# Placing the operands of TensorE at multiples of 512 bytes in an encoder layer with a mixer and 16,384 experts

## The chip, the core and the metric

The kernel runs on one core of one Trainium2 chip. The metric is the device time of one execution in microseconds, from runs of the same program; the kernel before took 2557.3 us in the median of three runs (2555.47 to 2557.51). A profiled execution gives a trace with every instruction's start and duration.

## What is computed

One encoder layer on 256 tokens of width 2048, in float32. The reference, cut to its matrix products:

```python
mod = silu(c) @ w_ada + b_ada
sh1, sc1, g1, sh2, sc2, g2 = split(mod, 6)
h = x * (1 + sc1) + sh1
proj = h @ w_in
...
x = layer_norm(ALPHA * x + g1 * (concat([y_ssd, y_sc]) @ w_out))
h = x * (1 + sc2) + sh2
q = h @ w_query
...
u_sel = take(expert_u, idx); act = gelu(einsum('tkd,td->tk', u_sel, h))
v_sel = take(expert_v, idx); ffn = einsum('tk,tkd->td', act * gate, v_sel)
x = layer_norm(ALPHA * x + g2 * ffn)
```

The mixer between `w_in` and `w_out` is a bidirectional state-space scan in 32 heads beside a gated short convolution. The experts are 128 x 128 single neurons; each token takes 16 in each of 8 heads.

## The kernel before, in words

All large products are made to float32 accuracy from float32r parts. `wsplit` (L71 to L84) loads 512 KB of weights as `raw` (128 x 1024), ScalarE (ACT) rounds it into `hi` (L78), VectorE (DVE) takes the rest, `lo = raw - hi` (L81). The activations are split the same way. `mm3` (L89 to L93) multiplies three times: `hi` by the high part (L91), `hi` by the low part (L92), `lo` by the high part (L93). In `mm3` the weights are the stationary operand (128 columns of float32, 512 bytes in each partition) and 256 tokens are the moving operand (1024 bytes). The text calls these narrow matmuls.

The stages follow each other:

- 0 to 256 us: `mod` on VectorE from streamed `w_ada`, and the first columns of `w_in` (`ps`, `ps_b`, 1632 narrow matmuls).
- 256 to 658 us: the rest of `w_in` (`ps_in`, 2304 narrow), with the scan and the convolutions between. Every third chunk of `WHOLE` does its first half in plain float32 (`proj_whole`, L101); such a matmul is recorded as two instructions.
- 658 to 863 us: `w_out` (`ps_o`, 1536 narrow), whose moving operands are the mixer's 64 tiles `y`, then the first layer norm.
- 863 to 1071.5 us: `w_query` (`ps_q`, 1536 narrow) with the top-16 search on VectorE; most weights of this stage go through the pool `s3`.
- 1071.5 to 1816 us: all 128 groups of 128 experts are multiplied densely with `h` (`ps_u`, 6144 narrow matmuls). Up to about 1467 us the gates are spread over the experts beside this: one-hot tiles `eq`, scaled into `o2` on ScalarE, and two matmuls `ps_g` (L814) after each 24 narrow ones.
- 1816 us to the end: `expert_v` (`ps_v`, L878, L879, L881). Here the activations `ah`, `al` are stationary (512 bytes) and 512 columns of `hi` or `lo` are moving (2048 bytes): 3072 wide matmuls. Then the second layer norm.

Tiles come from pools. A pool opened on the left takes the next free bytes from the bottom of SBUF, one opened with `side="right"` from the top; each tile begins at a multiple of 32 bytes. `const` is opened first, `stream` (the buffers `raw`, `hi`, `lo` of most stages) next, so the sizes of the small tiles in `const` set where `stream` and all that lies above it begin. `h2p` (`h2h`, `h2l`, the split `h`) and `wk5` (`ah`, `al`) are at the top. A scheduler orders the instructions of each engine; SyncE (SP) issues all large DMAs in one queue.

Of the kernel before, what the change touches and what calls it, by code (L numbers as in the profile page):

```python
# [7 lines left out]
F32 = mybir.dt.float32  # L8
# [10 lines left out]
P = 128  # L19
S = 256  # L20
D = 2048
ND = D // P
# [18 lines left out]
def layer_kernel(ctx, tc, I, out, dbg=None):  # L41
    nc = tc.nc
    V, A, G, T = nc.vector, nc.scalar, nc.gpsimd, nc.tensor

    def dump(name, ap):
        if dbg and name in dbg:
            nc.sync.dma_start(dbg[name], ap)

    def pool(stack, name, bufs=1, **kw):
        return stack.enter_context(tc.tile_pool(name=name, bufs=bufs, reuse_waits="tile", **kw))  # L50

    const = pool(ctx, "const")
# [8 lines left out]

    iota = const.tile([P, NE], F32, name="iota")
    G.iota(iota, pattern=[[1, NE]], base=0, channel_multiplier=0, allow_small_or_imprecise_dtypes=True)
    eps_t = const.tile([P, 1], F32, name="eps_t")
    V.memset(eps_t, EPS)
    badaT = const.tile([P, 6, ND], F32, name="badaT")
    mod = const.tile([P, 6, ND], F32, name="mod")
# [62 lines left out]
    def log(dst, src):  # L130
        log_tables()
        with tc.issue_after(tables.ins):
            A.activation(dst, src, AF.Ln)
# [10 lines left out]
        return sq.ins, V.scalar_tensor_tensor(r, t, 1.5, r, op0=ALU.add, op1=ALU.mult).ins  # L144


    macc = const.tile([P, 2, 2, ND], F32, name="macc")

    def ada_half(scb, w, part, d, half):

        cs = slice(half * 1024, (half + 1) * 1024)
        V.scalar_tensor_tensor(w, w, 0.5, scb[:, cs], op0=ALU.mult, op1=ALU.mult,  # L152
                               accum_out=macc[:, half, part % 2, d:d + 1])
# [66 lines left out]
    prm = pool(st2, "prm")  # L220
# [5 lines left out]
        return ys[chunk]  # L226

    scb = prm.tile([P, D], F32, name="scb")
    par = prm.tile([P, 194], F32, name="par")
    at = 0  # L230

    def load(n, shape=None):
        nonlocal at
        t = par[:, at:at + n]
        at += n
        return t if shape is None else t.rearrange("p (a b) -> p a b", a=shape)

    dtb, alog = load(1)[:64], load(1)[:64]
    cw = load(72, 24)
    cb = load(24)  # L240
    scw = load(48, 16)
# [7 lines left out]

    H = 64  # L250
    acT = prm.tile([P, 2, H], F32, name="acT")
    lnT = prm.tile([P, 2, H], F32, name="lnT")
    nbT = prm.tile([P, 2, H], F32, name="nbT")
    offT = prm.tile([P, H], F32, name="offT")

# [31 lines left out]
        xt4.append(w0.tile([P, 4, S], F32, name="xt4", tag="xt4", bufs=2) if i < 2 else None)  # L287
    nc.sync.dma_start(xt4[0], I["xT"][:, 0:4])
    nc.sync.dma_start(par, I["par"])
    nc.sync.dma_start(lnp, I["lnp"])  # L290
    for half in range(2):
        cs = slice(half * 1024, (half + 1) * 1024)
# [49 lines left out]
    for d in range(ND):  # L342
# [6 lines left out]
        n = -(-len(units) // (4 - d % 4))  # L349
# [15 lines left out]
    wk = pool(st1, "wk", 2)  # L365

    def tmp(tag, shape=(P, S), bufs=2):
        return (wk if len(tag) > 2 else wkS).tile(list(shape), F32, name=tag, tag=tag, bufs=bufs)
# [76 lines left out]
    e1 = tmp("Emat", (P, 6, P))  # L445
# [3 lines left out]
    def dt_sums():  # L449
# [12 lines left out]
        V.scalar_tensor_tensor(dt, dt, 2.0, u, op0=ALU.mult, op1=ALU.mult)  # L462
        V.scalar_tensor_tensor(dt, xr, 0.0, dt, op0=ALU.max, op1=ALU.add)
        dump("dt", dt)
        aneg = prm.tile([H, 1], F32, name="aneg")
        A.activation(aneg, alog, AF.Exp)
        V.tensor_scalar(xr, dt, aneg, -1.0, op0=ALU.mult, op1=ALU.mult)

        V.tensor_scalar(u, dt, 1e-37, None, op0=ALU.max)
        log(u, u)  # L470
        adT = e1[:, 0:2, :H]
        yield
        yield
        for c in range(2):
# [27 lines left out]
        yield  # L502

    later.append(dt_sums())


# [129 lines left out]
    wk = pool(stK, "wk2", side="right")  # L636
# [34 lines left out]
    for d in range(ND):  # L671
        with tc.high_priority(offset=900):
            r = rT[:, d]
# [28 lines left out]
    gT = eTp.tile([P, 2, S], F32, name="gT")  # L702
    st3 = ExitStack()
    big = pool(st3, "big3")
    wk3 = pool(st3, "wk3", 2)
    s3 = pool(st3, "s3", 5)
    pq = pool(st3, "pq", 6, space=PSUM)
    psc = pool(st3, "psc", 2, space=PSUM)
    sk = big.tile([P, 8, 2, 2, NE], F32, name="sk")
# [16 lines left out]
    for h in range(8):  # L726
        qt = wk3.tile([P, 4, S], F32, name="qt", tag="qt")
        pss = [pq.tile([P, S], F32, name="ps_q", tag="pq") for _ in range(4)]
        for k in (range(0, 4, 4) if h == 0 else range(4)):
            n = 4 if h == 0 else 1  # L730
# [64 lines left out]
    with ExitStack() as p4:  # L795
# [32 lines left out]
        with ExitStack() as p4a:  # L828
            wk = pool(p4a, "wk4a", 2)
# [12 lines left out]
        wk = pool(p4, "wk4b")  # L842
# [13 lines left out]
    with ExitStack() as p5:  # L856
        wk = pool(p5, "wk5", side="right")
# [4 lines left out]
        nc.sync.dma_start(scb5, bass.AP(tensor=sc_d.tensor, offset=sc_d.offset, ap=[[0, P], [1, D]]))  # L862
        banks = [[pv.tile([P, 512], F32, name="ps_v", tag="pm") for _ in range(4)] for _ in range(2)]
        g2b = wk.tile([P, D], F32, name="g2b")
        st = wk.tile([P, 2, 16], F32, name="st")

        def a_pair(e2):
            ah = wk.tile([P, 2, S], F32R, name="ah", tag="ah", bufs=3)
# [107 lines left out]
def _layout(inp):  # L976
    import numpy as np

    n = {k: np.asarray(v) for k, v in inp.items()}
    r = {}  # L980
# [4 lines left out]
    r["w_ada"] = n["w_ada"][0].reshape(D, 6, ND, P).transpose(1, 2, 3, 0)  # L985
    r["c"] = n["c"]
    pad = lambda f, b: np.concatenate([f[0], b[0], np.zeros(64, f.dtype)])[:, None]
    r["par"] = np.concatenate([
        pad(n["dt_bias_f"], n["dt_bias_b"]), pad(n["a_log_f"], n["a_log_b"]),
        n["conv_ssd_w"][0].reshape(3, 24, P).transpose(2, 1, 0).reshape(P, 72), cols(n["conv_ssd_b"][0]),  # L990
        n["short_conv_w"][0].reshape(3, 16, P).transpose(2, 1, 0).reshape(P, 48),
        cols(np.repeat(n["d_skip"][0], 64)), cols(n["ssd_norm_g"][0]), cols(n["sc_norm_g"][0])], axis=1)
# [42 lines left out]
```

## Time and profile before

| | us |
|---|---|
| median of 3 runs | 2557.3 |
| lowest and highest run | 2555.47, 2557.51 |
| profiled execution | 2552.61 |
| its span, first to last instruction | 2550.7 |
| TensorE busy (95% of the span) | 2424.6 |
| VectorE busy (73%) | 1862.2 |
| ScalarE busy (54%) | 1381.3 |

The mean granted TensorE clock of the profiled execution is 0.984 of full speed. Busy times of engines overlap. Records of consecutive matmuls overlap as well: one takes 0.28 us from start to end while the next starts after 0.11 us, so the pace of TensorE is read from starts, first and last of a stretch with their count, and not from durations.

### The profile page before, as it was taken

The numbers are of one execution on the slowest core, as the hardware profiler recorded it, in microseconds if no ns is written. First come the engines' busy times: TensorE is split into PE (matmuls) and PEld (weight loads), VectorE is DVE, ScalarE is ACT, GpSimd is POOL, SyncE is SP. The second block draws the span as 40 slices with busy tenths as digits, with TensorE's granted clock in tenths as the row PEclk, the third lists the DMA queues.
The fourth block names the chain that finished last, engine by engine and source line by source line (L and its number), as shares of the span: only waits on it lengthen the run. The fifth ranks groups of instructions, "written<-read, shape, count | busy, mean of one in ns | idle before, by whom it ended". The sixth has DMA issues, their size and how long they took to land.

```text
span 2550.7 us, 44290 instructions
## 1 busy us (share of the span) xinstructions
PE 2424.6 (95%) x17122; PEld 2248.3 (88%) x17122; DVE 1862.2 (73%) x3255; ACT 1381.3 (54%) x2506; POOL 0.9 (0%) x7
## 2 busy tenths in 40 slices
PE   5889999999999899999999999999998999999997
PEld 5889888888899799999999999999886888888886
DVE  8788888989887799898888855555675555645545
ACT  3435476656444554499999944444443444544442
POOL 0000000000000000000000000000000000000000
PEclk9999999999999899999999999999999999999999
DMA  9886766778887565355666666666788655655554
GB/s 356 313 297 236 260 217 224 235 260 280 267 291 259 196 206 181 116 181 193 199 195 200 198 218 219 218 217 219 257 307 274 217 194 190 223 192 193 193 190 149
DMA packets 183252, 575.67 MB, mean 226 GB/s; under 512 B 22209, under 2 KB 44929, under 8 KB 182657
## 3 DMA queue, kind: packets, MB, share of 16 engines
q1 hardware_dynamic: 183042, 572.85, 67.3%
q8 instruction: 134, 2.20, 0.3%
q14 instruction: 76, 0.62, 0.1%
HBM read 560.10 MB, written 12.66 MB: 225 GB/s over the span
## 4 chain that ended last, share of the span: by engine, by line
PE 67%; DMA 15%; DVE 12%; ACT 3%; issue 2%; SPq 1%; DVEq 0%; ACTq 0%
PE ps_u L91 9%; PE ps_u L92 9%; PE ps_u L93 9%; PE ps_v L879 8%; PE ps_v L881 8%; PE ps_v L878 8%; DVE lo L81 5%; DMA adaw<-in_w_ada_dram 4%; DMA raw<-in_w_in_dram 3%; DMA big<-in_w_ada_dram 2%; ACT hi L78 2%; DVE adaw L152 2%; DMA raw<-in_w_inA_dram 2%; PE ps_q L93 2%; PE ps_q L92 2%
## 5 line engine op out<-in xcount | busy, mean ns | idle before, releaser
L81 DVE TENSOR_TENSOR lo<-raw,hi 128x1024 fp32r<-128x1024 f32 (+1 forms) x804 | 972.1, 1212 | 506.8 <-ACT hi L78 504.7
L78 ACT ACTIVATE hi<-raw 128x1024 fp32r<-128x1024 f32 (+1 forms) x804 | 843.6, 1051 | 884.6 <-PE ps_v L879 302.1
L91 PE MATMUL ps_u<-h2h,hi 128*128 128x256 f32 x2048 | 568.7, 278 | 0.0
L92 PE MATMUL ps_u<-h2l,hi 128*128 128x256 f32 x2048 | 568.1, 277 | 0.0
L93 PE MATMUL ps_u<-h2h,lo 128*128 128x256 f32 x2048 | 568.1, 277 | 0.0
L878 PE MATMUL ps_v<-hi,ah 128*128 128x512 f32 x992 | 390.1, 393 | 9.9 <-ACT hi L78 8.1
L879 PE MATMUL ps_v<-hi,al 128*128 128x512 f32 x992 | 390.7, 394 | 1.2 <-DVE al L120 1.2
L91 PEld LDWEIGHTS ps_u<-h2h,hi 128*128 128x128 f32 x2048 | 386.2, 189 | 0.0
L92 PEld LDWEIGHTS ps_u<-h2l,hi 128*128 128x128 f32 x2048 | 384.6, 188 | 0.0
L93 PEld LDWEIGHTS ps_u<-h2h,lo 128*128 128x128 f32 x2048 | 384.5, 188 | 0.0
L881 PE MATMUL ps_v<-lo,ah 128*128 128x512 f32 x992 | 268.9, 393 | 0.8 <-DVE lo L81 0.8
L878 PEld LDWEIGHTS ps_v<-hi,ah 128*128 128x128 f32 x992 | 187.5, 189 | 52.3 <-ACT hi L78 8.9
L879 PEld LDWEIGHTS ps_v<-hi,al 128*128 128x128 f32 x992 | 187.7, 189 | 43.0 <-DVE al L120 1.6
L91 PE MATMUL ps_in<-h2h,hi 128*128 128x256 f32 x768 | 222.3, 289 | 3.0 <-DVE mod L159 2.2
L881 PEld LDWEIGHTS ps_v<-lo,ah 128*128 128x128 f32 x992 | 186.8, 189 | 42.0 <-DVE lo L81 2.0
L93 PE MATMUL ps_in<-h2h,lo 128*128 128x256 f32 x768 | 217.6, 283 | 2.3 <-DVE lo L81 2.3
L152 DVE SCALAR_TENSOR_TENSOR adaw<-adaw,scb 128x1024 f32<-128x1024 f32 x160 | 193.1, 1219 | 35.3 <-DMA adaw<-in_w_ada_dram 35.0
L92 PE MATMUL ps_in<-h2l,hi 128*128 128x256 f32 x768 | 217.6, 283 | 0.0
L809 ACT ACTIVATE o<-eq,gT 128x128 fp32r<-128x128 f32 x512 | 161.4, 388 | 0.0
L91 PEld LDWEIGHTS ps_in<-h2h,hi 128*128 128x128 f32 x768 | 146.6, 191 | 9.0 <-issue 4.2
L93 PEld LDWEIGHTS ps_in<-h2h,lo 128*128 128x128 f32 x768 | 147.1, 191 | 4.6 <-DVE lo L81 2.9
L93 PE MATMUL ps_o<-y,lo 128*128 128x256 f32 x512 | 145.6, 284 | 5.0 <-DVE lo L81 4.9
(285 smaller groups left out, 3975.0 us busy)
## 6 DMA issues: line engine op xcount, KB each, us to landing
raw<-in_expert_u_dram SPq DMA_DIRECT2D x256, 512.0 KB, 4.5
raw<-in_expert_v_dram SPq DMA_DIRECT2D x248, 512.0 KB, 3.9
adaw<-in_w_ada_dram SPq DMA_DIRECT2D x160, 512.0 KB, 6.0
raw<-in_w_in_dram SPq DMA_DIRECT2D x110, 512.0 KB, 5.0
raw<-in_w_out_dram SPq DMA_DIRECT2D x64, 512.0 KB, 4.3
raw<-in_w_query_dram SPq DMA_DIRECT2D x64, 512.0 KB, 3.9
raw<-in_w_inB_dram SPq DMA_DIRECT2D x44, 512.0 KB, 4.4
big<-in_w_ada_dram SPq DMA_DIRECT2D x32, 512.0 KB, 5.6
```

The costliest lines, as they stand in the source:

```text
L78: A.activation(hi, raw, AF.Copy)
L81: V.tensor_tensor(lo, raw, hi.bitcast(F32), op=ALU.subtract)
L91: T.matmul(ps, wh, mh, start=start, stop=False)
L92: T.matmul(ps, wh, ml, start=False, stop=False)
L93: T.matmul(ps, wl, mh, start=False, stop=stop)
L152: V.scalar_tensor_tensor(w, w, 0.5, scb[:, cs], op0=ALU.mult, op1=ALU.mult, accum_out=macc[:, half, part % 2, d:d + 1])
L809: A.activation(o2[:, k], eq[:, i, 1].bitcast(F32), AF.Copy, scale=gT[:, k, t0 + i:t0 + i + 1])
L878: T.matmul(banks[tb][c], ah[:, ts], vh, start=start, stop=False)
L879: T.matmul(banks[tb][c], al[:, ts], vh, start=False, stop=False)
L881: T.matmul(banks[tb][c], ah[:, ts], vl, start=False, stop=stop)
```

## The change

The small tiles `macc`, `eps_t`, the two vectors of the step size (`dtb`, `alog`) and `aneg` become parts of one tile `top` of 120 floats, in a pool of its own at the upper end of SBUF. The two vectors leave the input `par` and arrive by a DMA of their own, `dtp`. `lnT` moves into the unused half of `e1`, `st` grows from 16 to 64 columns, and pool `s3` is opened ahead of `wk3`. No arithmetic changes.

```diff
--- before.py
+++ after.py
@@ -61,7 +61,9 @@
 
     iota = const.tile([P, NE], F32, name="iota")
     G.iota(iota, pattern=[[1, NE]], base=0, channel_multiplier=0, allow_small_or_imprecise_dtypes=True)
-    eps_t = const.tile([P, 1], F32, name="eps_t")
+
+    top = pool(ctx, "top", side="right").tile([P, 120], F32, name="top")
+    macc, eps_t, dtp = top[:, :64].rearrange("p (h a d) -> p h a d", h=2, a=2), top[:, 64:65], top[:, 72:74]
     V.memset(eps_t, EPS)
     badaT = const.tile([P, 6, ND], F32, name="badaT")
     mod = const.tile([P, 6, ND], F32, name="mod")
@@ -144,8 +146,6 @@
         return sq.ins, V.scalar_tensor_tensor(r, t, 1.5, r, op0=ALU.add, op1=ALU.mult).ins
 
 
-    macc = const.tile([P, 2, 2, ND], F32, name="macc")
-
     def ada_half(scb, w, part, d, half):
 
         cs = slice(half * 1024, (half + 1) * 1024)
@@ -226,7 +226,7 @@
         return ys[chunk]
 
     scb = prm.tile([P, D], F32, name="scb")
-    par = prm.tile([P, 194], F32, name="par")
+    par = prm.tile([P, 192], F32, name="par")
     at = 0
 
     def load(n, shape=None):
@@ -235,7 +235,7 @@
         at += n
         return t if shape is None else t.rearrange("p (a b) -> p a b", a=shape)
 
-    dtb, alog = load(1)[:64], load(1)[:64]
+    dtb, alog = dtp[:64, 0:1], dtp[:64, 1:2]
     cw = load(72, 24)
     cb = load(24)
     scw = load(48, 16)
@@ -249,7 +249,6 @@
 
     H = 64
     acT = prm.tile([P, 2, H], F32, name="acT")
-    lnT = prm.tile([P, 2, H], F32, name="lnT")
     nbT = prm.tile([P, 2, H], F32, name="nbT")
     offT = prm.tile([P, H], F32, name="offT")
 
@@ -287,6 +286,7 @@
         xt4.append(w0.tile([P, 4, S], F32, name="xt4", tag="xt4", bufs=2) if i < 2 else None)
     nc.sync.dma_start(xt4[0], I["xT"][:, 0:4])
     nc.sync.dma_start(par, I["par"])
+    nc.sync.dma_start(dtp, I["dtp"])
     nc.sync.dma_start(lnp, I["lnp"])
     for half in range(2):
         cs = slice(half * 1024, (half + 1) * 1024)
@@ -462,13 +462,13 @@
         V.scalar_tensor_tensor(dt, dt, 2.0, u, op0=ALU.mult, op1=ALU.mult)
         V.scalar_tensor_tensor(dt, xr, 0.0, dt, op0=ALU.max, op1=ALU.add)
         dump("dt", dt)
-        aneg = prm.tile([H, 1], F32, name="aneg")
+        aneg = top[:H, 80:81]
         A.activation(aneg, alog, AF.Exp)
         V.tensor_scalar(xr, dt, aneg, -1.0, op0=ALU.mult, op1=ALU.mult)
 
         V.tensor_scalar(u, dt, 1e-37, None, op0=ALU.max)
         log(u, u)
-        adT = e1[:, 0:2, :H]
+        adT, lnT = e1[:, 0:2, :H], e1[:, 0:2, H:]
         yield
         yield
         for c in range(2):
@@ -702,8 +702,8 @@
     gT = eTp.tile([P, 2, S], F32, name="gT")
     st3 = ExitStack()
     big = pool(st3, "big3")
+    s3 = pool(st3, "s3", 5)
     wk3 = pool(st3, "wk3", 2)
-    s3 = pool(st3, "s3", 5)
     pq = pool(st3, "pq", 6, space=PSUM)
     psc = pool(st3, "psc", 2, space=PSUM)
     sk = big.tile([P, 8, 2, 2, NE], F32, name="sk")
@@ -862,7 +862,7 @@
         nc.sync.dma_start(scb5, bass.AP(tensor=sc_d.tensor, offset=sc_d.offset, ap=[[0, P], [1, D]]))
         banks = [[pv.tile([P, 512], F32, name="ps_v", tag="pm") for _ in range(4)] for _ in range(2)]
         g2b = wk.tile([P, D], F32, name="g2b")
-        st = wk.tile([P, 2, 16], F32, name="st")
+        st = wk.tile([P, 2, 64], F32, name="st")
 
         def a_pair(e2):
             ah = wk.tile([P, 2, S], F32R, name="ah", tag="ah", bufs=3)
@@ -985,8 +985,8 @@
     r["w_ada"] = n["w_ada"][0].reshape(D, 6, ND, P).transpose(1, 2, 3, 0)
     r["c"] = n["c"]
     pad = lambda f, b: np.concatenate([f[0], b[0], np.zeros(64, f.dtype)])[:, None]
+    r["dtp"] = np.concatenate([pad(n["dt_bias_f"], n["dt_bias_b"]), pad(n["a_log_f"], n["a_log_b"])], axis=1)
     r["par"] = np.concatenate([
-        pad(n["dt_bias_f"], n["dt_bias_b"]), pad(n["a_log_f"], n["a_log_b"]),
         n["conv_ssd_w"][0].reshape(3, 24, P).transpose(2, 1, 0).reshape(P, 72), cols(n["conv_ssd_b"][0]),
         n["short_conv_w"][0].reshape(3, 16, P).transpose(2, 1, 0).reshape(P, 48),
         cols(np.repeat(n["d_skip"][0], 64)), cols(n["ssd_norm_g"][0]), cols(n["sc_norm_g"][0])], axis=1)
```

Where the two built programs place the tiles, as the start in a partition modulo 512 bytes:

| tile | before | changed |
|---|---|---|
| `raw`, `hi`, `lo` of pool `stream` (moving in `ps_v`, else stationary) | 288 | 0 |
| `raw`, `hi`, `lo` of pool `s3` (most of `ps_q`) | 32 | 0 |
| `h2h`, `h2l` (moving in `ps`, `ps_b`, `ps_in`, `ps_q`, `ps_u`) | 480 | 0 |
| `y` (moving in `ps_o`), `h2w` (moving in L101) | 352 | 0 |
| `ah`, `al` (stationary in `ps_v`) | 480 | 0 |
| `eq` (stationary) and `o2` (moving) in `ps_g` | 288 | 0 |
| `rT` | 224 | 256 |

TensorE's instructions stand in the same order in both programs; so do, names apart, those of VectorE and of POOL. Two places differ. On the DMA queue of SP, at the start of the program (`adaw` are the first tiles of `w_ada`, `xt` the first tile of `x`), before:

```order
L281 DMA adaw_145<-in_w_ada_dram 128x1024 x2
L284 DMA badaT<-in_b_adaT_dram 128x96
L288 DMA xt_149<-in_xT_dram 128x1024
L289 DMA par<-in_par_dram 128x194
L290 DMA lnp<-in_lnp_dram 128x32
L296 DMA sc_d<-scb 1x2048
```

And with the change:

```order
L280 DMA adaw_146<-in_w_ada_dram 128x1024 x2
L283 DMA badaT<-in_b_adaT_dram 128x96
L287 DMA xt_150<-in_xT_dram 128x1024
L288 DMA par<-in_par_dram 128x192
L289 DMA top<-in_dtp_dram 128x2
L290 DMA lnp<-in_lnp_dram 128x32
L296 DMA sc_d<-scb 1x2048
```

One DMA is added ahead of `lnp`; `par` is two floats shorter in each partition. On ScalarE, just after the first tile of `h` (`h2w` is `h` in float32, `top` at L466 is `aneg`), before:

```order
L294 ACTIVATE lo<-scb 128x1024 x2
L314 ACTIVATE h2w_129<-xt_149,mod 128x256
L466 ACTIVATE aneg<-par 64x1
L119 ACTIVATE h2h<-h2w_129 128x256
L128 ACT_TABLE_LOAD
```

And with the change:

```order
L294 ACTIVATE lo<-scb 128x1024 x2
L314 ACTIVATE h2w_130<-xt_150,mod 128x256
L121 ACTIVATE h2h<-h2w_130 128x256
L466 ACTIVATE top<-top 64x1
L130 ACT_TABLE_LOAD
```

The exponential of 64 numbers stands one place later, behind the first rounding.

## Rows read from the trace of the kernel before

**Rows 1.** The page: span, busy time by engine, the chain that ended last by engine.
```profile
span 2550.7 us, 44290 instructions
...
PE 2424.6 (95%) x17122; PEld 2248.3 (88%) x17122; DVE 1862.2 (73%) x3255; ACT 1381.3 (54%) x2506; POOL 0.9 (0%) x7
...
PE 67%; DMA 15%; DVE 12%; ACT 3%; issue 2%; SPq 1%; DVEq 0%; ACTq 0%
```

**Rows 2.** Windows by stage: length, then busy us (xinstructions), granted clock, DMA share.
```profile
core 0: us, PE busy (x) PEld busy (x) DVE busy (x) ACT busy (x) POOL busy (x), PEclk, DMA share, GB/s
0.00:256.00 256.00, 210.01 (x1640) 201.00 (x1641) 208.85 (x369) 109.23 (x163) 0.63 (x6) 0.97 0.83 300
256.00:658.00 402.00, 375.52 (x2767) 346.57 (x2766) 353.60 (x685) 254.93 (x541) 0.00 (x0) 0.97 0.73 246
658.00:863.00 205.00, 189.48 (x1548) 186.14 (x1546) 153.46 (x258) 88.28 (x118) 0.24 (x1) 0.97 0.80 266
863.00:1071.50 208.50, 198.51 (x1679) 196.44 (x1680) 197.23 (x653) 101.75 (x181) 0.00 (x0) 0.98 0.52 173
1071.50:1467.00 395.50, 393.05 (x3351) 389.92 (x3350) 339.51 (x588) 363.04 (x972) 0.00 (x0) 1.00 0.59 190
1467.00:1816.00 349.00, 348.64 (x3076) 348.44 (x3075) 200.26 (x257) 154.25 (x196) 0.00 (x0) 1.00 0.68 218
1816.00:2550.70 734.70, 709.39 (x3072) 579.79 (x3072) 409.29 (x448) 309.78 (x340) 0.00 (x0) 0.98 0.65 215
```

**Rows 3.** Instructions on tile ps_u, 1470 to 1810 us; third column first and last start.
```profile
L93 PE MATMUL ps_u<-h2h,lo x1001: 276/276/276, 1469.9 to 1809.9; 128*128 128x256 f32 x167
```

**Rows 4.** Instructions on tile ps_o, 802 to 855 us.
```profile
L93 PE MATMUL ps_o<-y,lo x150: 279/279/279, 801.8 to 854.4; 128*128 128x256 f32 x150
```

**Rows 5.** Instructions on tile ps_q, 978 to 996 us and 1004 to 1021 us.
```profile
L93 PE MATMUL ps_q<-h2h,lo x54: 276/276/276, 977.8 to 995.8; 128*128 128x256 f32 x54
...
L93 PE MATMUL ps_q<-h2h,lo x48: 281/281/281, 1004.0 to 1020.7; 128*128 128x256 f32 x48
```

**Rows 6.** Instructions on tile ps_v, 2100 to 2500 us.
```profile
L878 PE MATMUL ps_v<-hi,ah x584: 388/390/394, 2100.1 to 2499.7; 128*128 128x512 f32 x195
L879 PE MATMUL ps_v<-hi,al x584: 388/392/394, 2100.3 to 2499.9; 128*128 128x512 f32 x195
L881 PE MATMUL ps_v<-lo,ah x581: 388/394/394, 2099.8 to 2498.1; 128*128 128x512 f32 x194
```

**Rows 7.** Two windows at the lower clock, and timeline rows (start us, us) in each.
```profile
865.20:866.50 1.30, 1.30 (x8) 1.30 (x8) 1.30 (x4) 0.70 (x2) 0.00 (x0) 0.50 1.04 425
1823.60:1824.90 1.30, 1.30 (x4) 1.00 (x3) 0.54 (x1) 0.05 (x1) 0.00 (x0) 0.50 0.88 246
...
865.18 0.41 PE L93 MATMUL ps_q<-h2h,lo 128*128 128x256 f32 x1
...
866.46 0.41 PE L93 MATMUL ps_q<-h2h,lo 128*128 128x256 f32 x1
...
1824.06 0.63 PE L878 MATMUL ps_v<-hi,ah 128*128 128x512 f32 x1
1824.49 0.63 PE L879 MATMUL ps_v<-hi,al 128*128 128x512 f32 x1
```

**Rows 8.** The chain in order of time, 500 to 512 us: start, length, what.
```profile
506.89 3.45 PE ps_in L101 x16
```

**Rows 9.** Timeline of TensorE around a pair of gate matmuls, from 1301.18 us.
```profile
1301.18 0.28 PE L93 MATMUL ps_u<-h2h,lo 128*128 128x256 f32 x1
1301.29 0.39 PE L814 MATMUL ps_g<-o,eq 128*128 128x256 f32 x2
1301.53 0.28 PE L91 MATMUL ps_u<-h2h,hi 128*128 128x256 f32 x1
```

**Rows 10.** Groups by line on ACT, 900 to 1060 us, then 1500 to 1800 us.
```profile
L78 ACT ACTIVATE hi<-raw 128x1024 fp32r<-128x1024 f32 x52 | 55.0, 1059 | 45.5 <-PE ps_q L92 36.0 <-DMA raw<-in_w_query_dram 5.2 <-ACT qt L734 2.3
...
L78 ACT ACTIVATE hi<-raw 128x1024 fp32r<-128x1024 f32 x111 | 118.0, 1063 | 169.2 <-PE ps_u L92 167.6 <-DMA raw<-in_expert_u_dram 1.6
```

**Rows 11.** Timeline of the DMA queue, 6 to 9 us, and of ACT, 14 to 15 us.
```profile
6.40 0.33 SPq L290 DMA_DIRECT2D lnp<-in_lnp_dram  x1
8.75 0.30 SPq L296 DMA_DIRECT2D sc_d<-scb  x1
...
14.35 0.19 ACT L466 ACTIVATE aneg<-par 64x1 f32<-64x1 f32 x1
```

## Prediction, made before the changed kernel ran

> **What bounds the kernel now.** The page first: TensorE is busy for 95% of the span, and the chain that ended last is TensorE for 67%, DMA for 15% and VectorE for 12% [rows 1]. The windows by stage say where this average comes from [rows 2]. From 1467 us to the end TensorE is the bound alone: 348.6 of 349.0 us in the second part of the first expert product, then 709.4 of 734.7 us. From 1071.5 to 1467 us it has a companion, since ScalarE is busy for 363.0 of 395.5 us; in the query stage VectorE is busy for 197.2 of 208.5 us. In the three stages before, TensorE is idle for 46.0, 26.5 and 15.5 us, and DMA shares of 0.73 to 0.83 tell what it waits for. Gains in TensorE's pace come out whole only in the last two windows.
>
> Then the pace itself, read from first and last start with the count. Narrow matmuls (256 columns) follow each other on `ps_u` at 340.0 us / 1000 / 3 = 113.3 ns [rows 3], on `ps_o` at 52.6 / 149 / 3 = 117.7 ns [rows 4], and on `ps_q` at 113.2 ns in one stretch and 118.4 in another [rows 5]. Wide ones (512 columns, 1749 starts in 400.1 us) come every 228.9 ns [rows 6]. The columns alone would take 106.7 and 213.3 ns at 2.4 GHz. What is the rest? At the lower granted clock, 0.50 or 1.2 GHz, there is none: six narrow gaps take 1.28 us, 213.3 ns each, and a wide one takes 0.43 us, which is 512 columns and nothing else [rows 7]. At full clock the plain float32 matmuls of L101, which take 512 column times for 256 columns, come every 3.45 us / 16 = 215.6 ns [rows 8], only 2.3 ns over. So only streams that take a new float32 column in every cycle at 2.4 GHz pay more. With 2.3 ns as the unavoidable part, the floors are 109.0 ns narrow and 215.6 wide. Over them lie 4.3, 8.7 and 13.3 ns: one, two and three steps of some 4.4 ns.
>
> The reader should note two things. The moving tiles of `ps_o` start 352 bytes past a multiple of 512 and always pay two steps; `h2h` starts at 480 and pays one or two. That speaks for the address. But `ps_q` shows both paces with the same addresses, so the phase of loads against matmuls has a say too.
>
> **The change, part by part.** My reading: an operand that starts off a multiple of 512 touches one more 512-byte block than it needs, the moving and the stationary operand each, and each extra block can cost one step. A narrow matmul has two extra blocks and pays one or two steps; a wide one has two as well and pays three. With all starts at 0 the narrow ones come to 109.0 ns, the wide ones lose two of three steps and come to 220.0. No start at 0 is in this trace, so this is bounded only by the rows: at best the floor for both, and on the other side no gain or a loss (rivals).
>
> The sum, stage by stage, with the counts and busy times of [rows 2]:
>
> 1. 1467 to 1816 us: 3076 instructions x 4.3 ns = 13.2 us, whole.
> 2. 1816 us to the end: 3072 x 8.9 = 27.3 us, whole; 40.9 at the floor of 215.6.
> 3. 1071.5 to 1467 us: 395.5 us / 3351 = 118.0 ns for an instruction, waits and both paces together. At 109.0 it would be 365 us, 30 less, but ScalarE alone needs 363.0. It would have no slack for its gate work, so I take 20, which leaves it 97% busy.
> 4. 658 to 863 us: 1548 x 8.7 = 13.5 us. Up to about 800 us `w_ada` tiles compete for the DMA queue; I take two thirds, 9.
> 5. 256 to 658 us: 2304 narrow ones at 4.3 to 8.7 ns, on average 6.5, give 15 us; with VectorE at 88% and DMA at 0.73, half: 7.5. Behind a faster TensorE the raw weights are late next.
> 6. 863 to 1071.5 us: 1536 at 4.3 to 8.7 give 6.6 to 13.4 us, but VectorE (95% busy) is late next. I take 3.
> 7. Up to 256 us: 1632 x 6.5 = 10.6 us of TensorE time in a stage that waits for VectorE and DMA. I take 2.
>
> Together 82.0 us. Taking every stage at its upper end gives 13.2 + 40.9 + 30 + 13.5 + 15 + 13.4 + 10.6 = 137.
>
> The rest is near nothing. The added DMA `dtp` costs an issue of about 0.33 us like `lnp`'s; the queue is idle from 6.73 to 8.75 us behind `lnp` [rows 11], which hides it. Were that cover gone, 0.33 us would fall on the next loads of `w_ada`. `aneg`, 0.19 us [rows 11], runs after the first rounding instead of before it, which lets TensorE's first operand be ready no later. `lnT` in `e1`, the wider `st` and `s3` ahead of `wk3` add no instruction. That ScalarE and VectorE, or DMA, gain from rounder addresses too, I put at 0: the same ScalarE rounding takes 1059 ns on tiles at 32 (pool `s3`) and 1063 at 288 [rows 10], no sign of an effect.
>
> Against its own time the profiled execution would go from 2552.6 to 2470.6 us. The median of the runs, 2557.3, is 4.7 above that execution; on this scale the forecast is **2475 us**.
>
> **The rivals.** *Only one operand counts (faster, about 2509).* The weights may be fetched early enough that their extra block is free, or the other way round. Then a wide matmul loses one step, to 224.5 (3072 x 4.4 = 13.5 us), `ps_o` goes to 113.3 (4.5 after waits), the steady `ps_u` still reaches 109.0 if its one step is the one that goes (13.2), the mixed stretch gives 12, the other three 1.5, 3 and 1: 48.7 us in all. For it: `h2h` often pays one step with both its operands off. Against: three steps on wide matmuls are not explained by one operand. [...]
>
> *The start does not matter (no change, 2557).* The steps may be the price of feeding a column in every cycle, whatever its address; the absence at half the rate [rows 7, 8] fits that as well, and [rows 5] shows a pace changing with no address changed. Against it: `ps_o` keeps two steps through all its 150 groups of three [rows 4]. [...] That the change does not do what it says can be left out: the built program has all these tiles at 0.
>
> *Equal starts collide (slower, about 2622).* With the change moving and stationary operands start at the same place in their blocks. Ordered by the distance between the two starts before, the paces are: 448 (`ps_q`) and 192 (`ps_u`) one or two steps, 64 (`ps_o`) always two, and 0, which only the gate matmuls have (both at 288), two starts in 0.24 us, 120 ns each [rows 9]. If nearness is what costs, all narrow ones go to 120 and wide ones pay a fourth step: 3076 x 6.7 = 20.6 us, 3351 x 4.5 (from a mean of 115.5 between the two paces) = 15.1, 3072 x 4.4 = 13.5, 1548 x 2.3 = 3.6, then 7 in the query stage and 5 in `ps_in` after what VectorE and DMA hide: 65 us. It decides as soon as steady `ps_u` runs above 113.3. Against it: a pair of gate matmuls is also a change of operands and of accumulator, which could cost those nanoseconds by itself.
>
> **How the numbers follow.** 0.2%, 5 us, is what a measurement of this kernel can tell from no change. I give the forecast 0.40, one operand 0.26, no effect 0.18, collision 0.16; so faster 0.66, same 0.18, slower 0.16. The forecast's own range is 2440 to 2500: the low end adds to the 82 us the wide floor (13.6) and some 21 of the 41 us held back in the other stages. To hold 8 in 10 the range must reach over the second and third case and ends at 2562, the highest run plus the 5 us; the collision is left out.
>
> **What would show it right or wrong.** In the changed trace: starts on `ps_u` from the middle of its stage at 109 ns instead of 113.3 and no stretch at 117.7; `ps_o` at 109; wide matmuls near 220 (215.6 would be the best end, 224.5 the rival's, 233 the collision's); the last two windows shorter by 13 and 27 us, the mixed one by 20 with ScalarE then the busiest; the query stage nearly as long as before. The forecast is wrong if `ps_u` keeps 113.3 and 117.7, if the wide pace stays at 228.9, or if the gain appears in the first 256 us, where only DMA or VectorE could have made it.

## The result and the profile after

The change made the kernel slower: 2580.28 us in the median of four runs (2575.91 to 2583.03), against 2556.39 for four runs of the kernel before (2549.79 to 2557.51); the ratio is 1.0097, with a 95% interval of 1.0073 to 1.0121. The forecast of 2475 us had the wrong sign, and its range ended at 2562. The profiled execution took 2583.03 us, 30.4 more than that of before.

In the changed kernel the lines of `wsplit` and `mm3` stand two further down: `hi` is rounded in L80, `lo` taken in L83, the triple is L93, L94, L95, and `proj_whole` is L103. The page first: span, busy time by engine, the chain by engine.

```profile
span 2581.2 us, 44290 instructions
...
PE 2469.0 (96%) x17122; PEld 2298.3 (89%) x17122; DVE 1871.0 (72%) x3255; ACT 1393.9 (54%) x2506; POOL 0.9 (0%) x7
...
PE 69%; DMA 14%; DVE 11%; ACT 3%; issue 2%; SPq 1%; DVEq 0%; ACTq 0%
```

Beside [rows 1], TensorE took 44.4 us more for the same 17122 instructions. Where? These are the windows of the changed kernel, cut where the same work begins and ends as in [rows 2] (columns as there).

```profile
0.00:253.60 253.60, 212.09 (x1637) 203.64 (x1638) 210.35 (x370) 109.21 (x162) 0.63 (x6) 0.95 0.85 304
253.60:653.00 399.40, 382.58 (x2769) 354.46 (x2768) 354.32 (x685) 255.15 (x542) 0.00 (x0) 0.98 0.74 248
653.00:857.50 204.50, 190.06 (x1547) 186.53 (x1545) 152.18 (x256) 88.30 (x118) 0.24 (x1) 0.99 0.80 265
857.50:1073.00 215.50, 207.74 (x1679) 205.63 (x1680) 198.03 (x654) 102.85 (x182) 0.00 (x0) 0.97 0.52 168
1073.00:1480.00 407.00, 405.54 (x3354) 403.01 (x3353) 346.54 (x589) 374.66 (x973) 0.00 (x0) 1.00 0.57 185
1480.00:1849.50 369.50, 368.86 (x3074) 368.66 (x3073) 200.29 (x257) 154.14 (x195) 0.00 (x0) 1.00 0.64 206
1849.50:2581.20 731.70, 702.11 (x3072) 576.38 (x3072) 409.25 (x448) 309.59 (x340) 0.00 (x0) 0.99 0.66 216
```

Stage by stage the change is -2.4, -2.6, -0.5, +7.0, +11.5, +20.5 and -3.0 us, together the 30.5 by which the span grew. The loss lies in the three windows of `ps_q` and `ps_u`; `w_in` and `w_out` did not grow, and the wide matmuls at the end gained a little.

The pace explains it. Instructions on tile `ps_u` in the part without gates, and TensorE's timeline around a pair of gate matmuls:

```profile
L95 PE MATMUL ps_u<-h2h,lo x973: 283/283/283, 1490.0 to 1839.9; 128*128 128x256 f32 x195
```
```profile
1308.11 0.28 PE L95 MATMUL ps_u<-h2h,lo 128*128 128x256 f32 x1
1308.23 0.40 PE L814 MATMUL ps_g<-o,eq 128*128 128x256 f32 x2
1308.47 0.28 PE L93 MATMUL ps_u<-h2h,hi 128*128 128x256 f32 x1
...
1311.35 0.40 PE L814 MATMUL ps_g<-o,eq 128*128 128x256 f32 x2
```

The first row gives 349.9 / 972 / 3 = 120.0 ns where [rows 3] gave 113.3. In the second view 24 narrow matmuls take 1311.35 - 1308.47 = 2.88 us, 120.0 each, and the gate pair 0.24: the pace that only the gate matmuls had before [rows 9] is now that of every narrow matmul. The two paces of [rows 5] are gone too; instructions on tile `ps_q`, 1004 to 1010 us (6.1 / 17 / 3 = 119.6 ns by rounded ends, 119.9 in the mean of the stage):

```profile
L93 PE MATMUL ps_q<-h2h,hi x18: 283/283/283, 1003.8 to 1009.9; 128*128 128x256 f32 x18
```

The wide ones, in the same stretch as [rows 6]:

```profile
L879 PE MATMUL ps_v<-hi,al x590: 389/389/389, 2099.7 to 2500.0; 128*128 128x512 f32 x197
L878 PE MATMUL ps_v<-hi,ah x589: 389/389/389, 2099.9 to 2499.7; 128*128 128x512 f32 x197
L881 PE MATMUL ps_v<-lo,ah x588: 389/389/389, 2101.2 to 2499.0; 128*128 128x512 f32 x196
```

1767 starts in 400.3 us are 226.7 ns, 2.2 less than before, about 6.8 us over 3072. The window shrank by 3.0 only. In the groups of TensorE by line, where the last column is its idle time and what ended it, the rest has become waiting. First the kernel before, then the changed one:

```profile
L879 PE MATMUL ps_v<-hi,al 128*128 128x512 f32 x992 | 390.7, 394 | 1.2 <-DVE al L120 1.2
L878 PE MATMUL ps_v<-hi,ah 128*128 128x512 f32 x992 | 390.1, 393 | 9.9 <-ACT hi L78 8.1 <-ACT ah L119 1.8
L881 PE MATMUL ps_v<-lo,ah 128*128 128x512 f32 x992 | 268.9, 393 | 0.8 <-DVE lo L81 0.8
```

```profile
L878 PE MATMUL ps_v<-hi,ah 128*128 128x512 f32 x992 | 387.4, 391 | 11.0 <-ACT hi L80 9.1 <-ACT ah L121 1.8
L879 PE MATMUL ps_v<-hi,al 128*128 128x512 f32 x992 | 386.8, 390 | 1.2 <-DVE al L122 1.2
L881 PE MATMUL ps_v<-lo,ah 128*128 128x512 f32 x992 | 266.4, 390 | 4.2 <-DVE lo L83 4.2
```

The waits add up to 16.4 us, where these three groups waited 11.9 before. So 4.5 of 7.3 us of less busy time (709.4 to 702.1) went into waits for rounded weights.

Two things did not move. At the lower granted clock (0.50) narrow matmuls still come every 213.3 ns (3.20 us / 15 below, as in [rows 7]), and sixteen plain float32 ones take 3.46 us against the 3.45 of [rows 8]. First the timeline of the start of `ps_q`, then the chain in order of time.

```profile
860.26 0.41 PE L93 MATMUL ps_q<-h2h,hi 128*128 128x256 f32 x1
...
863.46 0.41 PE L93 MATMUL ps_q<-h2h,hi 128*128 128x256 f32 x1
```
```profile
502.18 3.46 PE ps_in L103 x16
```

Last, the added DMA. Timeline of the queue, and TensorE's first large matmul:

```profile
6.26 0.33 SPq L289 DMA_DIRECT2D top<-in_dtp_dram  x1
8.41 0.33 SPq L290 DMA_DIRECT2D lnp<-in_lnp_dram  x1
9.77 0.30 SPq L296 DMA_DIRECT2D sc_d<-scb  x1
10.95 3.00 SPq L280 DMA_DIRECT2D adaw<-in_w_ada_dram  x4
...
22.41 0.58 PE L93 MATMUL ps<-h2h,hi 128*128 128x256 f32 x1 [18.31 <-ACT hi L80]
```

`lnp` goes out 2.0 us and `sc_d` 1.0 us later than in [rows 11]. In the kernel before, the second group of four `w_ada` tiles was issued at 9.45, and that first matmul came at 20.88: 1.5 us each. The runs below bear out the direction, with sizes that vary: in the eleven traces with `dtp` `lnp` goes out at 8.03 to 8.65 us, these tiles at 10.57 to 11.23, and the first matmul comes at 21.4 to 23.1; in the three without it, at 6.03 to 6.40, 9.45 to 9.63 and 20.9 to 21.1. What holds `lnp` back is not shown. The first stage nevertheless ended no later.

### The profile page after: what moved, and what is told of

It is laid out like the page before. It is cut to its first block, busy times and chain, and to the rows that moved or that the text cites. A ratio compares the mean times of both kernels' runs of the same rounds, so it can differ in the third digit from the quotient of the medians.

```text
span 2581.2 us, 44290 instructions
## 1 busy us (share of the span) xinstructions
PE 2469.0 (96%) x17122; PEld 2298.3 (89%) x17122; DVE 1871.0 (72%) x3255; ACT 1393.9 (54%) x2506; POOL 0.9 (0%) x7
## 4 chain that ended last, share of the span: by engine, by line
PE 69%; DMA 14%; DVE 11%; ACT 3%; issue 2%; SPq 1%; DVEq 0%; ACTq 0%
PE ps_u L94 9%; PE ps_u L93 9%; PE ps_u L95 9%; PE ps_v L878 7%; PE ps_v L879 7%; PE ps_v L881 7%; DVE lo L83 4%; DMA adaw<-in_w_ada_dram 4%; DMA big<-in_w_ada_dram 3%; DMA raw<-in_w_in_dram 2%; DVE adaw L152 2%; PE ps_q L95 2%; PE ps_q L93 2%; PE ps_q L94 2%; ACT hi L80 2%
## 5 line engine op out<-in xcount | busy, mean ns | idle before, releaser
L83 DVE TENSOR_TENSOR lo<-raw,hi 128x1024 fp32r<-128x1024 f32 (+1 forms) x804 | 973.5, 1213 | 521.1 <-ACT hi L80 511.4
L80 ACT ACTIVATE hi<-raw 128x1024 fp32r<-128x1024 f32 (+1 forms) x804 | 842.8, 1050 | 918.5 <-PE ps_v L879 280.5
L93 PE MATMUL ps_u<-h2h,hi 128*128 128x256 f32 x2048 | 580.0, 283 | 0.0
L95 PE MATMUL ps_u<-h2h,lo 128*128 128x256 f32 x2048 | 579.5, 283 | 0.0
L94 PE MATMUL ps_u<-h2l,hi 128*128 128x256 f32 x2048 | 579.5, 283 | 0.0
L93 PEld LDWEIGHTS ps_u<-h2h,hi 128*128 128x128 f32 x2048 | 393.1, 192 | 0.0
L94 PEld LDWEIGHTS ps_u<-h2l,hi 128*128 128x128 f32 x2048 | 393.1, 192 | 0.0
L95 PEld LDWEIGHTS ps_u<-h2h,lo 128*128 128x128 f32 x2048 | 393.0, 192 | 0.0
L93 PE MATMUL ps_in<-h2h,hi 128*128 128x256 f32 x768 | 225.0, 293 | 2.6 <-DVE mod L159 2.1
L95 PE MATMUL ps_in<-h2h,lo 128*128 128x256 f32 x768 | 220.2, 287 | 0.8 <-DVE lo L83 0.8
L94 PE MATMUL ps_in<-h2l,hi 128*128 128x256 f32 x768 | 220.3, 287 | 0.0
L93 PEld LDWEIGHTS ps_in<-h2h,hi 128*128 128x128 f32 x768 | 148.7, 194 | 8.7 <-issue 3.8
L95 PE MATMUL ps_o<-y,lo 128*128 128x256 f32 x512 | 146.1, 286 | 6.4 <-DVE lo L83 6.4
L95 PEld LDWEIGHTS ps_in<-h2h,lo 128*128 128x128 f32 x768 | 148.7, 194 | 2.7 <-issue 1.5
```

The lines of the kernel that those rows point to most:

```text
L80: A.activation(hi, raw, AF.Copy)
L83: V.tensor_tensor(lo, raw, hi.bitcast(F32), op=ALU.subtract)
L93: T.matmul(ps, wh, mh, start=start, stop=False)
L94: T.matmul(ps, wh, ml, start=False, stop=False)
L95: T.matmul(ps, wl, mh, start=False, stop=stop)
```

## The experiments

Before the change the distance from the start of the stationary operand to that of the moving one was 192 bytes in `ps_u` (480 - 288), 64 in `ps_o`, 448 in `ps_q`, and 288 - 480 = -192 in the expert product at the end. After it all are 0. The theory after the result was that this **distance** decides, so that the loss is not in the multiples of 512 but in both operands having the same one. The rival: the start of each **by itself** decides, and a multiple of 512 is bad for narrow matmuls and good for wide ones. A third possibility was that neither counts and some other part of the change slowed the kernel. In the expectations these are theory D (distance), A (the start by itself) and N (the addresses do not matter).

Means below are over the gaps between successive starts in a stage, those over 140 ns (wide: 260) left out. Times of whole executions are compared only for t2, t3 and t4, which were repeated; the others serve for the paces.

**e1 to e3: the changed kernel with small unused tiles** that shift `y`, the buffers of `s3`, and `ah`/`al`; `h2h` and the buffers of `stream` stay at 0, so `ps_u` is unchanged in all. The edit of e1:

```diff
+    prm.tile([P, 16], F32, name="pad_y")
...
+    big.tile([P, 48], F32, name="pad_q")
...
+        pool(p5, "pad5", side="right").tile([P, 112], F32, name="pad_v")
```

In e2 the three widths are 32, 32, 96, in e3 48, 16, 64.

> The changed kernel with three groups of tiles moved off 0: y (moving in ps_o) to 64, the buffers of s3 (stationary in ps_q) to 192, ah and al (stationary in ps_v) to 64; all else stays at 0. Distance of the moving start from the stationary start, modulo 512: ps_o 64, ps_q 320, ps_v 448, ps_u 0. Theory D (the distance sets the pace, distance 0 is the worst): ps_o 117.8 ns as in the kernel before, which had the same distance at other addresses; ps_q below 120, at 113 to 118; ps_u stays at 120. Theory A (what costs is a start at 0 modulo 512 itself, of either operand): every stage still has one operand at 0 and at most one step goes, 115.6 to 120 in ps_o and ps_q alike, whatever the distance. Theory N (the addresses don't matter, the order of loads does): 120 everywhere.

> As the run before it, with y, s3, ah and al at 128. Distances: ps_o 128, ps_q 384, ps_v 384, ps_u 0. Theory D: ps_o and ps_q each have one pace from start to end, 109 to 118 ns, and not 120; the wide pace differs from 226.7 ns. Theory A: the same paces as in the run with 64 and 192, since only one operand is at 0 in both. Theory N: 120 and 226.7.

> As the two before, with y at 192, s3 at 64, ah and al at 256. Distances: ps_o 192, which ps_u had in the kernel before, ps_q 448, which ps_q had before, ps_v 256. Theory D: ps_o 113.3 or 117.8 ns, ps_q 113.3 or 118, both as before the change. Theory A: the same as in the two runs before. Theory N: 120.

Measured in e1 (instructions on tiles `ps_o`, `ps_v`, `ps_u`):

```profile
L95 PE MATMUL ps_o<-y,lo x142: 279/279/279, 801.8 to 851.6; 128*128 128x256 f32 x142
```
```profile
L881 PE MATMUL ps_v<-hi,ah x572: 398/398/398, 2100.3 to 2499.3; 128*128 128x512 f32 x191
```
```profile
L95 PE MATMUL ps_u<-h2h,lo x943: 283/283/283, 1470.1 to 1809.9; 128*128 128x256 f32 x189
```

`ps_o` at a distance of 64 is back at its old pace: 49.8 / 141 / 3 = 117.7 ns, as in [rows 4]. `ps_q` at 320 takes 117.9. The wide matmuls at 448 take 399.0 / 571 / 3 = 232.9, by the mean 233.3: slower than in either kernel. In e2, at 128 and 384, the narrow ones take 118.8 and the wide ones 232.6. In e3 `ps_o` at 192 runs partly at 113.3 and partly at 117.8 (mean 115.7), `ps_q` at 448 mostly at 113.3 (mean 114.1), and `ps_v` at 256 takes 226.9, as at 0. Instructions on `ps_q` in e3:

```profile
L95 PE MATMUL ps_q<-h2h,lo x12: 276/276/276, 1008.8 to 1012.5; 128*128 128x256 f32 x12
```

3.7 us / 11 / 3 is 112 ns by rounded ends, where the changed kernel has 120. So distances of 64 and 192 bring back the paces that they had before the change. One operand at a multiple of 512 is no harm: `h2h` stays at 0 in `ps_q`, which takes 114.1 ns in e3. Theory A as it was put down fails here: it expected one pace for all three runs, since one operand is at 0 in each, and `ps_o` took 117.4, 118.8 and 115.7 in the mean, `ps_q` 117.9, 118.8 and 114.1. A wider form of it, in which each other start has a price of its own, can still live with this.

**e4: equal starts away from 0.** The kernel before, with `y` and its weights both at 288, the weights of `ps_q` at 480 like `h2h`, and `ah`/`al` at 288 like the streamed buffers. `ps_u` keeps 480 and 288.

```diff
-    lnT = prm.tile([P, 2, H], F32, name="lnT")
+    prm.tile([P, 112], F32, name="pad_y")
...
-        adT = e1[:, 0:2, :H]
+        adT, lnT = e1[:, 0:2, :H], e1[:, 0:2, H:]
...
+    big.tile([P, 112], F32, name="pad_q")
...
+        pool(p5, "pad5", side="right").tile([P, 48], F32, name="pad_v")
```

> The kernel before, with starts made equal but not 0: y at 288 like the weights' buffers (ps_o distance 0), s3 at 480 like h2h (ps_q distance 0), ah and al at 288 like hi and lo (ps_v distance 0); ps_u keeps 480 against 288, distance 192. Theory D: ps_o and ps_q go to 120.0 ns and ps_v to 226.7, as with everything at 0, while ps_u keeps 113.3 and 117.8; the time is about 10 to 15 us above the kernel before. Theory A: ps_o and ps_q stay at 113 to 118 and ps_v at 229, the time stays at 2556. Theory N: as the kernel before.

Instructions on `ps_o`, `ps_u` and `ps_v`:

```profile
L91 PE MATMUL ps_o<-y,hi x40: 283/283/283, 834.8 to 848.9; 128*128 128x256 f32 x40
```
```profile
L93 PE MATMUL ps_u<-h2h,lo x1001: 276/276/276, 1469.8 to 1809.8; 128*128 128x256 f32 x167
```
```profile
L881 PE MATMUL ps_v<-hi,al x590: 389/389/389, 2099.7 to 2500.0; 128*128 128x512 f32 x197
```

Equal starts at 288 and 480 do the same as equal starts at 0: `ps_o` 14.1 / 39 / 3 = 120.5 by the row (119.9 by the mean), `ps_q` 119.9, `ps_v` 226.8, while `ps_u` stays at 113.3. No operand lies at a multiple of 512 here. This settles it for the distance and against the start by itself; and as the rest of the change is absent but for `lnT`, which lies in `e1` here too, nothing else in it is needed for the pace. The 10 to 15 us that were expected in the whole time are not shown: the run was made once, and between first and last start `ps_q` grew from 208.2 to 212.7 us while `ps_o` shrank from 196.3 to 194.5 and `ps_v` from 719.1 to 715.3.

**e5 to e8: the other distances, and the period.** The changed kernel with the three lines of e1 and the widths 24, 24, 120 (e5), 40, 8, 104 (e6), 56, 56, 88 (e7), and 64, 64, 72 (e8).

> The changed kernel with y at 96, the buffers of s3 at 96, ah and al at 32. Distances, modulo 256 (the runs so far gave the same pace for 64 and 320, for 128 and 384, and for 192 and 448): ps_o 96, ps_q 160, ps_v 224. Theory D with a period of 256 and a smooth course between the known points (64: 117.8, 128: 118.8, 192: 113.3 or 117.8 ns): ps_o 117 to 119, ps_q 113 to 119; wide between 233.3 (at 192) and 226.7 (at 0), so about 230. Theory L (a distance that is no multiple of 64 costs a step more, since lines are split): 120 or more in both, wide over 233.

> As the run before it with y at 160, s3 at 32, ah and al at 96. Distances modulo 256: ps_o 160, ps_q 224, ps_v 160. Theory D with a period of 256: ps_o has the pace of ps_q in the run with 96 (same distance, other stage), ps_q at 224 lies near 113 ns or below, wide 229 to 233. Theory L: 120 or more.

> As before with y and s3 at 224, ah and al at 160. Distances modulo 256: ps_o 224, ps_q 32, ps_v 96. Theory D with a period of 256: ps_o has the pace of ps_q in the run before, ps_q at 32 lies between 117.8 and 120, wide between 228.9 and 232.6. Theory L: 120 or more.

> As before with y and s3 at 256, ah and al at 224. Distances: ps_o 256, ps_q 256, ps_v 288. If the period is 256, ps_o and ps_q go to 120.0 ns like distance 0, and the wide pace, 32 modulo 256, lies between 226.7 and 228.9. If the period is 512 (and 64 and 320 agreed by chance), ps_o and ps_q lie well under 120.

Two rows on `ps_o`, first e5 at 96, then e8 at 256:

```profile
L95 PE MATMUL ps_o<-y,lo x40: 279/282/286, 834.7 to 848.8; 128*128 128x256 f32 x40
```
```profile
L94 PE MATMUL ps_o<-y,hi x40: 283/283/283, 834.8 to 848.8; 128*128 128x256 f32 x40
```

Both take 120 ns in the mean (119.95 and 119.9), but e5 with unequal gaps of 115 to 125 ns, and e8 in even steps like the changed kernel. A narrow distance of 256 acts as 0, as the wide one did in e3, so the table goes by the distance modulo 256. For narrow matmuls four pairs bear this out (0 and 256, 64 and 320, 128 and 384, 192 and 448), for wide ones the first pair alone. All measured means, in ns:

| distance mod 256 | narrow | wide |
|---|---|---|
| 0 | 119.9 to 120.0 (after, e4, e8) | 226.7 to 226.9 (after, e3, e4) |
| 32 | 116.9 (e7) | 233.3 (e8) |
| 64 | 117.4 to 117.9 (before, e1) | 228.9 (before) |
| 96 | 119.95 (e5) | 233.3 (e7) |
| 128 | 118.8 (e2) | 232.6 (e2) |
| 160 | 118.0 (e6), 118.3 (e5) | 234.3 (e6) |
| 192 | 114.1 to 115.7 (before, e3) | 233.3 (e1) |
| 224 | 118.3 (e6, e7) | 233.3 (e5) |

The smooth course between the known points, which the expectations assumed, is not there: 96 narrow was to take 117 to 119 ns, 224 narrow 113 or less, 32 narrow over 117.8, and wide ones at 224 and 32 about 230 and under 228.9. Nor does theory L hold, that a distance which is no multiple of 64 costs a step more: narrow matmuls at 32 are faster than at 64 (116.9 ns against 117.4 to 117.9), and the wide 233.3 of 32, 96 and 224 is also that of 192. It took split lines for the cause, which no run shows. The pace has to be measured for each distance.

For narrow matmuls 192 is best (113.3 ns on steady `ps_u` of the kernel before, which had this distance in `ps_u` and `ps_q`); 0 is at the bad end (120.0). For wide ones 0 is best (226.7), and the kernel before had the second best (228.9).

**t2: only `h2h` and `h2l` moved back to a distance of 192.** The changed kernel with `top` packed into 72 floats, which puts them at 192; a filler keeps `ah` and `al` at 0.

```diff
-    top = pool(ctx, "top", side="right").tile([P, 120], F32, name="top")
-    macc, eps_t, dtp = top[:, :64].rearrange("p (h a d) -> p h a d", h=2, a=2), top[:, 64:65], top[:, 72:74]
+    top = pool(ctx, "top", side="right").tile([P, 72], F32, name="top")
+    macc, eps_t, dtp = top[:, :64].rearrange("p (h a d) -> p h a d", h=2, a=2), top[:, 64:65], top[:, 65:67]
...
-        aneg = top[:H, 80:81]
+        aneg = top[:H, 68:69]
...
+        pool(p5, "pad5", side="right").tile([P, 48], F32, name="pad_v")
```

> The changed kernel with one thing undone: the tile top is packed from 120 to 72 floats, so that h2h and h2l begin 192 bytes past a multiple of 256 again, the distance that they had from the weights before; ah and al are held at 0, all else stays at 0. Theory D: ps_u, ps_in, ps_b and ps_q return to 113.3 and 117.8 ns, ps_o stays at 120.0, wide matmuls stay at 226.7; the time falls from 2580 to about 2552, a little under the kernel before (6.7 us less in ps_v, up to 3.4 more in ps_o), ratio 0.996 to 1.000. If the 24 us came from something else that the change did (the added DMA, pool places, DMA or VectorE on other addresses), the time stays near 2580, ratio 1.009.

2544.06 us in the median of 12 runs (before: 2551.97 in 29 runs), ratio 0.9959, interval 0.9941 to 0.9977 (the ratios are those on record, not quotients of the two medians). The windows of `ps_q`, of `ps_u` with and without gates, and of the end, then `ps_u`:

```profile
860.90:1067.80 206.90, 197.49 (x1679) 195.40 (x1680) 197.54 (x654) 101.77 (x182) 0.00 (x0) 0.98 0.52 173
1067.80:1463.90 396.10, 393.54 (x3355) 390.18 (x3354) 338.77 (x589) 360.17 (x973) 0.00 (x0) 1.00 0.59 190
1463.90:1812.50 348.60, 348.31 (x3074) 348.11 (x3072) 200.25 (x257) 153.91 (x195) 0.00 (x0) 1.00 0.69 218
1812.50:2542.50 730.00, 703.03 (x3072) 578.97 (x3072) 409.34 (x448) 310.17 (x340) 0.00 (x0) 0.98 0.66 216
```
```profile
L95 PE MATMUL ps_u<-h2h,lo x912: 276/276/276, 1489.9 to 1799.7; 128*128 128x256 f32 x183
```

309.8 / 911 / 3 = 113.4 ns: the pace is back, and the three windows that had lost 39 us are within 1.6 of [rows 2]. All other parts of the change are still there, so they cost nothing that these windows show; the wide gain is kept (734.7 to 730.0), and the kernel is faster than the one before.

**t3: t2 with `y` at 192 as well**, so that `ps_o` has its best distance too.

```diff
+    prm.tile([P, 48], F32, name="pad_y")
```

> The same with y moved to 192 as well, so that every narrow product of the projections and experts has distance 192 and the wide one 0. Theory D: ps_o 113.3 or 117.8 ns, mean about 115.7; 226.7 in ps_v; 7 to 10 us below the kernel before, ratio 0.996 to 0.998.

Instructions on `ps_o`:

```profile
L93 PE MATMUL ps_o<-y,hi x31: 276/276/276, 834.8 to 845.0; 128*128 128x256 f32 x31
```

113 ns by the row (10.2 / 30 / 3), 114.8 in the mean against 119.9 in t2, but its stage, from first to last start, only went from 195.7 to 194.0 us. What took up the rest is not shown for t3; in the changed kernel TensorE waits 6.4 us for `lo` from VectorE in this stage. The median is 2544.74 us, ratio 0.9981 (0.9963 to 0.9999): no further gain that can be measured.

**t4: the wide distance alone.** The kernel before with `ah` and `al` at 288.

```diff
+        pool(p5, "pad5", side="right").tile([P, 48], F32, name="pad_v")
```

> The kernel before with ah and al alone moved, from 480 to 288, equal to hi and lo modulo 512 but at no multiple of 512. Theory D: all narrow paces as before, ps_v at 226.7 instead of 228.9 ns, 3072 x 2.2 = 6.8 us less, ratio about 0.9975. If alignment to 512 were what helped ps_v, 228.9 and no change.

Instructions on `ps_v`:

```profile
L879 PE MATMUL ps_v<-hi,ah x589: 388/389/390, 2100.0 to 2499.9; 128*128 128x512 f32 x197
```

399.9 / 588 / 3 = 226.7 ns. The stage went from 719.1 to 714.7 us between first and last start, and the median is 2545.44, ratio 0.9971 (0.9953 to 0.9990). One line does what the whole change was able to gain, and again without a multiple of 512. Of the 6.5 us between the medians, 4.4 are seen in this stage.

**e9: which weights?** The changed kernel with `hi` of `s3` at 64 (a distance of 192) and `lo` at 256 (a distance of 0), to see whether the interval in which `lo` is used or the one in which it is loaded pays.

```diff
-            lo = pool.tile([P, 1024], F32R, name="lo", tag="lo")[:, :width]
+            lo = (pool.tile([P, 1152], F32R, name="lo", tag="lo")[:, 48:48 + width] if pool is not stream else
+                  pool.tile([P, 1024], F32R, name="lo", tag="lo")[:, :width])
...
+    big.tile([P, 16], F32, name="pad_q")
```

> The changed kernel with the buffers of s3 at two places: hi at 64 (distance 192 from h2h and h2l), lo at 256 (distance 0). In the query stage each triple then has two weight loads at distance 192 (before the first two of its matmuls) and one at 0 (before the third). Theory C (the load of the next weights runs beside the matmul, and the two reads disturb each other): the interval that begins with the second matmul, in which lo is loaded, is the slow one, 120 ns, the other two 113 to 118. Theory O (a matmul pays for its own weights): the interval that begins with the third matmul is the slow one. Every other stage as with the change.

Neither was seen over the stage. The gaps after the first, second and third matmul of a triple on `ps_q` are 118.1, 119.3 and 117.7 ns in the mean: all three moved, and none is the 120 beside two of 113 that either picture asks for. The second, during which `lo` is loaded, is the longest by 1.2 to 1.6 ns, but in e1, where `hi` and `lo` lie alike, it is the longest too, by 0.5. Only from 919 to 940 us do the three differ clearly, 121.6, 127.4 and 117.6: there the second is the slow one, as theory C has it, but so is the first. The run is inconclusive.

## Why the prediction was wrong

The step of the prediction that failed is the reading that opens "The change, part by part": that an operand off a multiple of 512 touches an extra 512-byte block, that each block can cost a step of some 4.4 ns, and that starts at 0 therefore bring 109.0 and 220.0 ns. It was the author's assumption, and no run shows such a block. The runs showed in its place that the distance of the two starts, modulo 256, sets the pace. The start itself has no say (e4: 120 and 226.8 with both operands at 288 or 480). The steps and their floor fall with it: means such as 116.9 and 118.8 ns lie between the steps, and the floors of 109.0 and 215.6, taken from plain float32, were reached at no distance; the best paces were 113.3 and 226.7. The column times of 106.7 and 213.3 ns are an estimate from [rows 7]: 256 columns in 213.3 ns at a granted clock of 0.50 are 1.2 in a nanosecond, and twice that at the full clock. At one column a cycle these are the 1.2 and 2.4 GHz of the prediction, which no trace shows as such. That an instruction of L101 takes 512 column times is in the same way an estimate, from its 215.6 ns [rows 8]. All four places of the forecast's sum that counted were built on it:

1. *`ps_u` without gates*: forecast -13.2 us, measured +20.5. 3074 instructions went from 113.3 to 120.0, and since TensorE has no companion there, 6.7 x 3074 = 20.6 us came out whole. That gains or losses of pace come out whole here was right.
2. *The wide matmuls*: forecast -27.3, measured -3.0. The pace fell by one half of a step (228.9 to 226.7), and of the 7.3 us of less work 4.5 turned into waits for `hi` and `lo`.
3. *`ps_u` with gates*: forecast -20, measured +11.5; not 15, since waits and the slower of the two paces lay in the 118.0 ns before (now 407.0 / 3354 = 121.3).
4. *`ps_o`, `ps_in`, `ps_q` and the first columns*: forecast -9, -7.5, -3 and -2; measured -0.5, -2.6, +7.0 and -2.4. That TensorE's pace does not set the length of the first two is right: `ps_o` went from 117.8 to 119.9 ns and `ps_in` from 115.0 to 119.3 without a longer stage. Before the change TensorE waits there for VectorE among others, 4.9 us for `lo` in the stage of `ps_o` and 11.6 us for `Emat` in that of `ps_in`. In `ps_q` VectorE was no cover for a loss: TensorE was already as busy as VectorE (198.5 and 197.2 of 208.5 us), so of 1536 x 5.6 = 8.6 us more, 7.0 came out.

The evidence was read in one way where two were open. `ps_o` "always pays two steps" because its distance is 64, not because it starts 352 past a multiple. That two paces can occur at one distance (192) misled as well; it is real (e3 has 113.3 and 117.8 ns on `ps_o`). The trace of before shows when it changes: from 1160 us to the end of the gates, each of the 101 groups of 24 narrow matmuls between two gate pairs has the other pace than the group ahead of it, 117.7 and 113.8 ns in turn, and in the part without gates, where no other matmuls come between, 113.3 stays. An interruption can flip the pace, with no address changed; by what means stays open.

The rival *equal starts collide* had the right condition, a distance of 0, the narrow price and the sign. Its 20.6 us for `ps_u` without gates were measured at 20.5, its 7 for `ps_q` at 7.0. It failed in the wide term: instead of a fourth step, 233.3 ns and +13.5 us, distance 0 is the best for wide matmuls. Without that term and the 5 us for `ps_in` its 65 us would be 46.5; the 30.5 measured are less again because the mixed stretch took 11.5 instead of 15.1 and the remaining stages gave 8.5 back instead of taking 3.6. Its nearness does not hold as a rule either: 96 is as slow as 0 for narrow matmuls (119.95 and 120.0 ns), and 32 faster than 64 (116.9 and 117.4 or more). It had 0.16, and the range left it out. [rows 9] held the number: two gate matmuls, the only ones at distance 0, 0.24 us for both.

*The start does not matter* is refuted by e1 to e4. Its sign that the excess exists only at a full column rate was right: distance 0 costs nothing at a granted clock of 0.50 (213.3 ns in both kernels) or in plain float32 (3.46 us for sixteen against 3.45). *Only one operand counts* falls too. The runs do not bear out that the two operands are independent: at a granted clock of 1.00 the place of the weights against the moving tile makes a narrow float32r matmul on `ps_u` take 113.3 ns (before; 113.4 in t2) or 120.0 (the changed kernel). Whether it is the weight load that costs is not shown (e9).

The small edits: `dtp` was put at 0.33 us, hidden. In fact the first matmul came 1.5 us later, and in the eleven traces with `dtp` it comes 0.3 us or more after the latest of the three without. The cover that was named, an idle queue behind `lnp`, was no cover, since `lnp` itself moved back by 2.0 us. It was absorbed in the rest of the first stage, whose end did not move later (253.6 us against 256.0).

Shown by runs are the dependence on the distance, for narrow matmuls its period of 256, and that `h2`'s place alone makes the loss. The writes of the other engines into the weights' buffers are not the cause: in the part of `ps_u` without gates of the changed kernel the gaps that begin while ScalarE is busy and those that begin while it is idle are both 120.0 ns in the mean (1153 and 1918 gaps), and it is the same with VectorE. That two reads collide is only argued: no run shows the reads. Why narrow and wide matmuls have different best distances stays open too.

## What to carry to other kernels

Before tiles are moved for the sake of alignment, work out for each large product where the moving and the stationary operand start relative to each other, and ask which pace of the present trace belongs to which distance; a kernel may sit on the best one without anyone having meant it. One padding tile per operand tells whether the place counts: measure the pace from starts in the stage where TensorE is alone, and do it for narrow and wide matmuls apart, since here they wanted different distances (192 for narrow ones, 113.3 ns; 0 for wide ones, 226.7). A change that helps one stage and hurts another is worth splitting, as here, where the one half lost some 39 us and the other alone gained 6.5 by the medians (t4).

## What the runs showed that was not expected

- The pace of float32r matmuls at the full granted clock depends on the distance of the operands' starts modulo 256 bytes: 113.3 to 120.0 ns for 256 columns, 226.7 to 234.3 for 512, by no simple course between.
- At distance 0 the gaps are even (5978 of 6121 on `ps_u` read 120 ns, and the wide ones 226 or 227); at distances such as 96 they are unequal, 115 to 125 ns, with the same mean.
- At a distance of 192 the narrow pace has two values, 113.3 and 117.8 ns, and a pair of other matmuls in between can flip it (117.7 and 113.8 in turn from group to group in the kernel before).
- A short DMA ahead of others on SyncE's queue took 0.33 us to issue, but in eleven traces with it the next loads of `w_ada` go out 0.9 to 1.8 us later than in the three without.
